# A two-layer encoder on one Trainium2 core: rotary products and weight folds pinned in VectorE's program order, folds in quarters, evictions with priority

## The chip, the core and the metric

The kernel runs on one core of a Trainium2 chip. The core has a matrix engine (TensorE, PE in the profile; its weight loads are listed apart as PEld), a vector engine (VectorE, DVE), a scalar engine (ScalarE, ACT), a slow general engine (GpSimd, POOL) and a sync engine (SyncE, SP), which here only issues DMA transfers. Each engine works through its own list of instructions in order, and the engines wait for one another by semaphores. The metric is the device time of one execution in microseconds (us), the median of several runs.

## What is computed

The reference is a two-layer bidirectional encoder over 272 tokens (16 learned tokens and 256 of input) with a model width of 2048. Cut to what matters:

```python
for i in range(2):
    h = _rmsnorm(h_stream, norm_mix[i])
    proj = h @ w_in[i]                       # q | k | v | f | ga | gf
    q = _rope_2d(_rmsnorm(q, q_norm[i]), ...)
    k = _rope_2d(_rmsnorm(k, k_norm[i]), ...)
    attn = softmax(q k^T / sqrt(128)) v      # 8 query heads, 2 key heads
    a_br = attn @ w_attn_br[i]
    fr = fft2(f by groups of 128 channels, axes=(positions, channels)).real
    s_br = fr @ w_four[i]
    merged = sigmoid(ga) * a_br + sigmoid(gf) * s_br
    h_stream = h_stream + merged @ w_out[i]
    up = _rmsnorm(h_stream, norm_ffn[i]) @ w_up[i]
    u_gate = dwconv3(up[..., :5632]); u_val = up[..., 5632:]
    h_stream = h_stream + (silu(u_gate) * u_val) @ w_down[i]
```

## The kernel before, in words

**Layout.** Activations lie with channels on the 128 partitions and the 272 tokens along the row. Weights come from memory in chunks of 512 KB (`raw`, 128 x 1024 fp32 numbers: four slices of 128 rows by 256 columns), through SyncE's queue at L179 into 4 buffers. Each chunk is split for the matrix engine in two parts, a rounded one and the rest: ScalarE casts `wh` from `raw` (L213), then VectorE computes `wl` = `raw` - `wh` (L214). There are 3 buffers each for `wh` and `wl`. Activations are split in the same way, and PE does three products for each block: `wh` with both activation parts, `wl` with the high one. There are 850 such chunks.

**What runs over what.** `group` (L242 on) works through one block of 256 output columns: for each chunk it splits ahead by two chunks (`LOOK`), then issues the matmuls into accumulators in PSUM, of which the tags `mm` and `aux` have 4 buffers each. Between matmuls, `step` takes one piece of work from a list of generators (`shadow`), which is how the attention, the rotary products and the folds of weights are woven into the stream of matmuls; the numbers that generators yield say how many steps to let pass before the next piece.

**Who decides the order.** The program text is an order of its own, but a scheduler then orders each engine's instructions by priority (by default the place in the text) and by when it reckons an instruction to be ready. A later instruction can therefore be put ahead of an earlier one of the same engine. `tc.keep_in_program_order(ins)` adds a dependence on the instruction of the same engine that stands just ahead in the text, so the instruction cannot be put ahead of that. `tc.high_priority(offset=150)` gives the instructions inside it the priority of a place 150 further up.

**Layer 1's folded projection.** The Fourier branch of layer 1 uses the symmetry of the transform: sums and differences of pairs of weight slices (`fw`, kept in device memory) meet sums and differences of mirrored tokens. `prefold` (L427) makes `fw` beforehand, during the feed-forward part of layer 0: for each of 32 chunks it loads a chunk `pfi` (L433), computes two halves of `pfo`, one sum and one difference of 128 x 512 numbers (L441), and stores `pfo` to `fw` (L435). Both transfers go through SyncE's queue, among the weight chunks. Layer 1 reads `fw` as 16 weight chunks in `folded_f` (L661 on), whose loop over k is the 16 chunks: four groups of two accumulators each (`ps_f`), L679 and L683 for `wh` and `wl`, L682 for a few channels apart. Groups 2 and 3 use the same four PSUM buffers as the q groups. At the last k the accumulators are evicted to `E` (L687, L688). `fold_pair` (L640 to L653) prepares the folded activations `hA` and `hB`, some of them while `folded_f` runs.

**Queries.** The q projection comes in four groups of two heads (i = 0 to 3). In layer 1 the folded projection runs between the second and the third. After each group `head_evac` evicts PSUM: ScalarE squares into `qps` (L745), VectorE scales into `qp` (L746). `q_stage` then takes sums of squares, starts `swap`, four transfers on SyncE's queue (L759) which copy `qp` with its 32-partition blocks exchanged into `qs`, waits some steps and runs `rope`:

- L763: `qs` = `qs` * sin, which needs the four transfers;
- L764: `qp` = `qp` * cos, in place;
- L765: `qp` = `qp` + `qs`;
- L766 on ScalarE and L767 on VectorE: the split of the result into its two parts.

**Attention.** `attention` (L883 on) goes through nine blocks of queries for each key head: scores (L906), maximum (L908), exponential on ScalarE (L913), normalisation on VectorE (L918, L921, L922), transposes on PE (L930) and the products with the values (L952). It begins once the first two q groups are rotated and the Fourier tokens are done, in layer 1 while the third q group and the gates are projected. The exponential needs ScalarE's table loaded, which is a listed instruction of its own at L913. A one-number tile `warm` is written by an activation at the program's start (L374).

Of the kernel before, what the change touches and what calls it, by code (L numbers as in the profile page):

```python
# [2 lines left out]

# [1 line left out]

# [7 lines left out]
AF = mybir.ActivationFunctionType  # L13
ALU = mybir.AluOpType
AX = mybir.AxisListType

P = 128
# [5 lines left out]
KT = D // P  # L23
# [24 lines left out]
TH = T // 2 + 2  # L48
# [13 lines left out]
P_QN = P_BG + DEPTH * 2 * KT  # L62
# [61 lines left out]
def _rep(ap, n):  # L124
    return ap.unsqueeze(1).to_broadcast([ap.shape[0], n, ap.shape[1]])
# [3 lines left out]
def encoder_kernel(ctx, tc, xT, params, consts, bmat, cfold, csign, w_fl, w_f64c, w_in, w_abr, w_four, w_f64, w_out, w_up, w_down, outT):  # L129
    nc = tc.nc  # L130
# [53 lines left out]
    def advance(upto):  # L184
        while st["raw"] < min(upto + RAW, len(chunks)):
            load_raw(st["raw"])
            st["raw"] += 1
        while st["fetch"] < min(upto, len(chunks)):
            i = st["fetch"]
            if i in folded:  # L190
                todo.append((i, lambda i=i: fold_w(i)))
            todo.append((i, lambda i=i: split_w(i, 0, CW)))
            st["fetch"] += 1

    def pump(upto=None):
        if upto is None:
            if todo:
                todo.pop(0)[1]()
        while upto is not None and todo and todo[0][0] <= upto:
            todo.pop(0)[1]()  # L200
# [153 lines left out]
    prm = per.tile([P, P_N], F32, name="prm")  # L354
    cst = per.tile([P, C_N], F32, name="cst")
    ones = per.tile([P, P], F32, name="ones")
    warm = per.tile([P, 1], F32, name="warm")
    mhalf = per.tile([P, 24], F32, name="mhalf")
# [35 lines left out]
    sin = cst[:, C_SIN:C_SIN + T]  # L394
# [7 lines left out]
    def bc2(ap):  # L402
        return _rep(ap, 2)
# [23 lines left out]
    def prefold(pool):  # L427
        src = [w_fl[k] for k in range(KT)] + [w_four[1, j, c] for j in range(NG) for c in range(2)]
        outs = {}
        for j in range(len(src) + 1):  # L430
            if j < len(src):
                a = pool.tile([P, CW, MG * P], F32, tag="pfi", name=f"pfi{j}", bufs=2)
                nc.sync.dma_start(a, src[j])  # L433
            if j:
                nc.sync.dma_start(fw[j - 1], outs.pop(j - 1))  # L435
            yield 12
            if j < len(src):
                o = pool.tile([P, CW, MG * P], F32, tag="pfo", name=f"pfo{j}", bufs=2)
                half = (lambda t_, q: t_[:, :, q * P:(q + 1) * P]) if j < KT else (lambda t_, q: t_[:, 2 * q:2 * q + 2])
                for q, op in ((0, ALU.add), (1, ALU.subtract)):  # L440
                    nc.vector.tensor_tensor(half(o, q), half(a, 0), half(a, 1), op=op)  # L441
                    yield 3
                outs[j] = o
            yield 12

    def norm_stats(holder):
        ps = psum.tile([P, 512], F32, tag="aux", name="ps_nst")
# [25 lines left out]
    for l in range(DEPTH):  # L473
        last = l == DEPTH - 1
        lo = 14 if last else 0
# [4 lines left out]
        with tc.tile_pool(name=f"mix{l}", bufs=1) as mp:  # L480
            E = mp.tile([P, 4, 2, TH] if last else [P, NG, T], F32, tag="q1b" if last else "q1", name="E")
            e64 = mp.tile([2 * NG, TH], F32, tag="u", name="e64", bufs=2) if last else None
# [15 lines left out]
            def rt(name):  # L498
                return mp.tile([P, 2, 2 * TH], F32, tag="r", name=name, bufs=7)[:, :, :T]
# [86 lines left out]
            if l == 0:  # L586
# [18 lines left out]
                ps = group((l, "f", 2), xr(0), T, "aux")  # L605
# [55 lines left out]
            def folded_f(slots, E):  # L661
                assert order[st["grp"]][0] == (l, "f4")
                st["grp"] += 1
                ps = {}
                for g in (0, 1, 2, 3):
                    ps[g] = [psum.tile([P, 512], F32, tag="aux" if g < 2 else "mm", name=f"ps_f{g}{e}") for e in range(2)]
                p64 = ps[0][0][:2 * NG, 2 * TH:3 * TH]
                for k in range(KT):
                    i = st["next"]
                    advance(i + 1 + LOOK)  # L670
                    pump(i)
                    h, lo_ = splits.pop(i)
                    st["next"] += 1
                    sl = slots[k % NS]
                    for g in ((2, 3, 0, 1) if k == KT - 1 else (0, 1, 2, 3)):
                        for e in range(2):
                            w = slice(e * P, (e + 1) * P)
                            o2 = ps[g][e][:, :2 * TH].rearrange("p (r n) -> p r n", r=2)
                            nc.tensor.matmul(o2, h[:, g, w], sl[:, e], start=k == 0, stop=False)  # L679
                            if g == e == 0:  # L680
                                for r in range(2):
                                    nc.tensor.matmul(p64, w64s[:, k, :], sl[:, 0, r, :], start=False, stop=False)  # L682
                            nc.tensor.matmul(ps[g][e][:, :TH], lo_[:, g, w], sl[:, e, 0, :], start=False, stop=k == KT - 1)  # L683
                        pump()
                        if k == KT - 1:
                            for e in range(2):
                                nc.scalar.copy(E[:, g, e, :], ps[g][e][:, TH:2 * TH])  # L687
                                nc.vector.tensor_tensor(E[:, g, e, :], ps[g][e][:, :TH], E[:, g, e, :], op=ALU.add)  # L688
                            if g == 0:
                                nc.scalar.copy(e64, p64)  # L690
                    if k % 2 and k + NS < KT:
                        fold_pair((k + NS - 1) // 2, slots)

# [43 lines left out]
            def head_evac(ps, gcol, name, lo):  # L737
                hp = rt(name)
                sq = rt(name + "s")
                if lo:  # L740
                    nc.gpsimd.memset(hp[:, :, 0:lo], 0.0)
                    nc.gpsimd.memset(sq[:, :, 0:lo], 0.0)
                for m in range(MG):
                    x = ps[m][:, :T - lo]
                    nc.scalar.activation(sq[:, m, lo:T], x, AF.Square)  # L745
                    nc.vector.scalar_tensor_tensor(hp[:, m, lo:T], x, gcol, rstdB[:, lo:T], op0=ALU.mult, op1=ALU.mult)  # L746
                return hp, sq
# [12 lines left out]
                return qs  # L760

            def rope(hp, qs, H, L):
                nc.vector.tensor_tensor(qs, qs, bc2(sin), op=ALU.mult)  # L763
                nc.vector.tensor_tensor(hp, hp, bc2(cos), op=ALU.mult)  # L764
                nc.vector.tensor_tensor(hp, hp, qs, op=ALU.add)  # L765
                nc.scalar.copy(H, hp)  # L766
                nc.vector.tensor_tensor(L, hp, H.bitcast(F32), op=ALU.subtract)  # L767
# [6 lines left out]
            ps = group((l, "k", 0), xr(0), T)  # L774
# [37 lines left out]
            ps = group((l, "v", 0), xr(0), T)  # L812
# [168 lines left out]
            qH, qL = [], []  # L981
            for i in range(4):
                ps = group((l, "q", i), xr(lo), W)
                qq = head_evac(ps, prm[:, P_QN + l:P_QN + l + 1], "qp", lo)
                if last:
                    if i in (0, 2):
                        until(hold, "vt" if i == 0 else "fold")
                        for t_, n in ((qH, "q1"), (qL, "q2")):
                            t_.append(mp.tile([P, 4, T], F32R, tag=n + "ab"[i // 2], name=n))
                elif i == 0:  # L990
                    until(hold, "vt")
                    until(hold, "fold")
                    for t_, n in ((qH, "q1"), (qL, "q2")):
                        t = mp.tile([P, NH, T], F32R, tag=n, name=n)
                        t_ += [t[:, 0:4], t[:, 4:8]]
                push(q_stage(i, *qq), 4)
                if last and i == 1:
                    until(hold, "ahead")
                    folded_f(slots, E)
                    o1_tiles()  # L1000
                    push(folded_chan(E), 1)
# [14 lines left out]
            for half in range(2):  # L1016
                mH = mL = None
                for kind, i in BRANCH_ORDER[half]:
                    j = i - 4 * half
# [18 lines left out]
                    else:  # L1038
# [6 lines left out]
                        ps = group((l, "a", i), lambda kt: (qH[kt // 4][:, kt % 4, lo:T], qL[kt // 4][:, kt % 4, lo:T]), W)  # L1045
                        for m in range(MG):
                            k = 2 * j + m
                            t_, h_ = tha[i][:, m, lo:T], mH[:, k, lo:T]
# [4 lines left out]
                for mg in range(8):  # L1053
                    ps = group((l, "o", half, mg), lambda kt: (mH[:, kt, lo:T], mL[:, kt, lo:T]), W)
# [7 lines left out]
        with tc.tile_pool(name=f"ffn{l}", bufs=1) as fp:  # L1062
# [6 lines left out]
            for c, n in enumerate(FF_SPLIT):  # L1069
                gHL = fp.tile([P, FF_SPLIT[0], 2, T], F32R, tag="gHL", name="gHL")  # L1070
                gH, gL = gHL[:, :, 0, :], gHL[:, :, 1, :]
                for i in range(k0 // MG, (k0 + n) // MG):
                    ps = group((l, "ug", i), xr(lo), W)
                    until(hold, "tok2")
                    cs = []
                    for m in range(MG):
# [7 lines left out]
                        a = max(lo2, 1)  # L1084
# [5 lines left out]
                    ps = group((l, "uv", i), (lambda kt: (xHL[:, kt, :, lo2:T],)) if fused else xr(lo2), W2)  # L1090
                    for m in range(MG):
                        j = 2 * i + m - k0
# [11 lines left out]
                for mg in range(8):  # L1104
                    two = fused and not (lastc and mg == 7)
                    ps = group((l, "d", c, mg), (lambda kt: (gHL[:, kt, :, lo2:T],)) if two
                               else (lambda kt: (gH[:, kt, lo2:T], gL[:, kt, lo2:T])), W2)
# [78 lines left out]
```

## Time and profile before

| what | us |
|---|---|
| median of three runs | 2589.75 |
| lowest and highest of the three | 2589.42, 2589.86 |
| the profiled execution, its own time | 2590.24 |
| span of the profiled execution (first to last instruction) | 2588.5 |
| one cast `wh` (L213), mean of 850 | 1.046 |
| one `wl` (L214), mean of 850 | 1.222 |
| memory traffic over the span | 493 MB, 191 GB/s |

How to read the views: a row of a timeline is the start in us, the duration in us, the engine, the line, the operation, the tiles written and read with their shapes, and in brackets the time for which the engine stood idle before it and what ended that. A row of a list of groups gives the count, the busy time and the mean of one instruction in ns, and then the idle time before them. A row of a list of waits gives the engine and line that waited, the engine and line that ended the wait, and the total, the number and the longest of these waits. "Granted clock" is the share of full speed at which PE was allowed to run.

### The profile page before, as it was taken

The page shows a single profiled execution, that of the slowest core. Times are in us where ns is not written, and L with a number is a line of the kernel's source. Part 1 is how long each engine was busy: PE and PEld are TensorE (multiplying, and loading weights), DVE is VectorE, ACT ScalarE, POOL GpSimd, SP SyncE. Part 2 cuts the span into 40 slices and gives each one's busy share as a digit, 9 for nine tenths or more (in the row PEclk, how much of TensorE's full clock was granted, in tenths as well). Part 3 has the DMA queues.
Part 4 walks back from the last instruction along what each step waited for, and adds up shares of the span by engine and source line. Part 5 has one row for each costly group of instructions (what it writes and reads, how often), then busy time and mean ns, then how long its engine had stood idle before and what let it go on. Part 6 is the DMA issues. An engine that isn't in the chain of part 4 may idle for free.

```text
span 2588.5 us, 47816 instructions
## 1 busy us (share of the span) xinstructions
PE 2570.9 (99%) x19604; PEld 2503.6 (97%) x19604; DVE 1720.3 (66%) x2742; ACT 1215.5 (47%) x1762; POOL 19.5 (1%) x40
## 2 busy tenths in 40 slices
PE   9999999999999999999999999999999999999999
PEld 9999999999999999999998999999999998899988
DVE  7787766777765445565567777667766665566654
ACT  5455434554444334444445555445544543354443
POOL 0000000000000000000000000000000000000000
PEclk9999999999999999999999999999999999999999
DMA  7545555589985555555556446566555555555564
GB/s 234 168 148 164 186 183 186 183 288 323 315 284 178 173 178 171 178 173 177 173 164 206 146 146 199 189 194 191 184 184 187 187 187 188 187 183 186 186 199 158
DMA packets 142811, 499.20 MB, mean 193 GB/s; under 512 B 16368, under 2 KB 23152, under 8 KB 142592
## 3 DMA queue, kind: packets, MB, share of 16 engines
q1 hardware_dynamic: 140144, 494.02, 58.1%
q8 instruction: 153, 2.51, 0.4%
q10 hardware_dynamic: 2448, 2.13, 0.2%
q14 instruction: 66, 0.54, 0.1%
HBM read 474.43 MB, written 18.87 MB: 191 GB/s over the span
## 4 chain that ended last, share of the span: by engine, by line
PE 92%; DVE 3%; DMA 3%; ACT 1%; issue 1%; SPq 0%; POOL 0%; DVEq 0%; ACTq 0%
PE ps_uv L266 6%; PE ps_ug L271 6%; PE ps_ug L272 6%; PE ps_ug L270 6%; PE ps_d L266 6%; PE ps_d L270 4%; PE ps_d L271 4%; PE ps_d L272 4%; PE ps_uv L267 3%; PE ps_d L267 3%; PE ps_uv L272 3%; PE ps_uv L270 3%; PE ps_uv L271 3%; PE ps_gf L270 2%; PE ps_gf L271 2%; PE ps_o L271 2%
## 5 line engine op out<-in xcount | busy, mean ns | idle before, releaser
L214 DVE TENSOR_TENSOR wl<-raw,wh 128x1024 fp32r<-128x1024 f32 (+1 forms) x850 | 1036.1, 1222 | 676.7 <-ACT wh L213 671.0
L213 ACT CAST wh<-raw 128x1024 fp32r<-128x1024 f32 (+1 forms) x850 | 887.7, 1046 | 989.9 <-issue 156.3
L271 PE MATMUL ps_ug<-xHL,wh 128*128 128x272 f32 (+1 forms) x1408 | 402.4, 286 | 0.0
L272 PE MATMUL ps_ug<-xHL,wl 128*128 128x272 f32 (+1 forms) x1408 | 402.2, 286 | 0.1
L270 PE MATMUL ps_ug<-xHL,wh 128*128 128x272 f32 (+1 forms) x1408 | 402.0, 286 | 0.0
L270 PEld LDWEIGHTS ps_ug<-xHL,wh 128*128 128x128 f32 x1408 | 265.4, 189 | 1.0
L272 PEld LDWEIGHTS ps_ug<-xHL,wl 128*128 128x128 f32 x1408 | 265.0, 188 | 0.7 <-DVE wl L214 0.7
L271 PEld LDWEIGHTS ps_ug<-xHL,wh 128*128 128x128 f32 x1408 | 265.5, 189 | 0.1
L266 PE MATMUL ps_uv<-xHL,wh 128*128 128x512 f32 x704 | 247.7, 395 | 0.0
L266 PE MATMUL ps_d<-gHL,wh 128*128 128x512 f32 x664 | 233.1, 395 | 0.0
L271 PE MATMUL ps_d<-gHL,wh 128*128 128x272 f32 (+1 forms) x744 | 214.4, 288 | 0.0
L270 PE MATMUL ps_d<-gHL,wh 128*128 128x272 f32 (+1 forms) x744 | 214.1, 288 | 0.0
L272 PE MATMUL ps_d<-gHL,wl 128*128 128x272 f32 (+1 forms) x744 | 214.0, 288 | 0.0
L272 PE MATMUL ps_uv<-xHL,wl 128*128 128x272 f32 x704 | 203.2, 289 | 0.6 <-DVE wl L214 0.5
L271 PE MATMUL ps_uv<-xHL,wh 128*128 128x272 f32 x704 | 203.0, 288 | 0.0
L270 PE MATMUL ps_uv<-xHL,wh 128*128 128x272 f32 x704 | 202.9, 288 | 0.0
L267 PE MATMUL ps_uv<-xHL,wl 128*128 128x256 f32 x704 | 197.7, 281 | 0.0
L267 PE MATMUL ps_d<-gHL,wl 128*128 128x256 f32 x664 | 186.5, 281 | 0.0
L266 PEld LDWEIGHTS ps_uv<-xHL,wh 128*128 128x128 f32 x704 | 132.4, 188 | 29.9
L266 PEld LDWEIGHTS ps_d<-gHL,wh 128*128 128x128 f32 x664 | 125.0, 188 | 29.2
L270 PE MATMUL ps_ga<-xHL,wh 128*128 128x272 f32 (+1 forms) x512 | 148.0, 289 | 0.0
L270 PE MATMUL ps_gf<-xHL,wh 128*128 128x272 f32 (+1 forms) x512 | 147.3, 288 | 0.0
(321 smaller groups left out, 5854.7 us busy)
## 6 DMA issues: line engine op xcount, KB each, us to landing
raw<-in_w_up SPq DMA_DIRECT2D x352, 512.0 KB, 3.5
raw<-in_w_in SPq DMA_DIRECT2D x191, 512.0 KB, 3.6
raw<-in_w_down SPq DMA_DIRECT2D x176, 512.0 KB, 3.5
raw<-in_w_out SPq DMA_DIRECT2D x64, 512.0 KB, 3.5
raw<-in_w_abr SPq DMA_DIRECT2D x32, 512.0 KB, 3.5
fw<-pfo SPq DMA_DIRECT2D x32, 512.0 KB, 6.4
raw<-fw SPq DMA_DIRECT2D x32, 512.0 KB, 3.6
raw<-in_w_four SPq DMA_DIRECT2D x16, 512.0 KB, 3.7
```

Of the source, the lines that this page charges most:

```text
L213: nc.scalar.copy(h[:, a:b], r[:, a:b])
L214: nc.vector.tensor_tensor(lo[:, a:b], r[:, a:b], h[:, a:b].bitcast(F32), op=ALU.subtract)
L266: nc.tensor.matmul(o2, h[:, c, sl], ab, start=kt == 0, stop=False)
L267: nc.tensor.matmul(o, lo[:, c, sl], ab[:, 0, :], start=False, stop=kt == nk - 1)
L270: nc.tensor.matmul(o, h[:, c, sl], a, start=kt == 0, stop=False)
L271: nc.tensor.matmul(o, h[:, c, sl], b, start=False, stop=False)
L272: nc.tensor.matmul(o, lo[:, c, sl], a, start=False, stop=kt == nk - 1)
```

## The change

It has five parts: `prefold` works in quarters (128 x 256 numbers) in place of halves, each one pinned, with other numbers of steps between the pieces; the evictions to `E` and, for the second q group of layer 1, those of `head_evac` stand under `high_priority`; the first rotary product is pinned; and an exponential on the one-number tile `warm` is issued at k = 2 of `folded_f`.

```diff
--- before.py
+++ after.py
@@ -1,5 +1,5 @@
 import math
-from contextlib import ExitStack
+from contextlib import ExitStack, nullcontext
 
 import numpy as np
 
@@ -433,15 +433,16 @@
                 nc.sync.dma_start(a, src[j])
             if j:
                 nc.sync.dma_start(fw[j - 1], outs.pop(j - 1))
-            yield 12
+            yield 15
             if j < len(src):
                 o = pool.tile([P, CW, MG * P], F32, tag="pfo", name=f"pfo{j}", bufs=2)
-                half = (lambda t_, q: t_[:, :, q * P:(q + 1) * P]) if j < KT else (lambda t_, q: t_[:, 2 * q:2 * q + 2])
                 for q, op in ((0, ALU.add), (1, ALU.subtract)):
-                    nc.vector.tensor_tensor(half(o, q), half(a, 0), half(a, 1), op=op)
-                    yield 3
+                    for c in range(2):
+                        half = (lambda t_, e: t_[:, 2 * c:2 * c + 2, e * P:(e + 1) * P]) if j < KT else (lambda t_, e: t_[:, 2 * e + c])
+                        tc.keep_in_program_order(nc.vector.tensor_tensor(half(o, q), half(a, 0), half(a, 1), op=op))
+                        yield 3
                 outs[j] = o
-            yield 12
+            yield 1
 
     def norm_stats(holder):
         ps = psum.tile([P, 512], F32, tag="aux", name="ps_nst")
@@ -683,11 +684,14 @@
                             nc.tensor.matmul(ps[g][e][:, :TH], lo_[:, g, w], sl[:, e, 0, :], start=False, stop=k == KT - 1)
                         pump()
                         if k == KT - 1:
-                            for e in range(2):
-                                nc.scalar.copy(E[:, g, e, :], ps[g][e][:, TH:2 * TH])
-                                nc.vector.tensor_tensor(E[:, g, e, :], ps[g][e][:, :TH], E[:, g, e, :], op=ALU.add)
-                            if g == 0:
-                                nc.scalar.copy(e64, p64)
+                            with tc.high_priority(offset=150):
+                                for e in range(2):
+                                    nc.scalar.copy(E[:, g, e, :], ps[g][e][:, TH:2 * TH])
+                                    nc.vector.tensor_tensor(E[:, g, e, :], ps[g][e][:, :TH], E[:, g, e, :], op=ALU.add)
+                                if g == 0:
+                                    nc.scalar.copy(e64, p64)
+                    if k == 2:
+                        nc.scalar.activation(warm, mhalf[:, 0:1], AF.Exp)
                     if k % 2 and k + NS < KT:
                         fold_pair((k + NS - 1) // 2, slots)
 
@@ -760,7 +764,7 @@
                 return qs
 
             def rope(hp, qs, H, L):
-                nc.vector.tensor_tensor(qs, qs, bc2(sin), op=ALU.mult)
+                tc.keep_in_program_order(nc.vector.tensor_tensor(qs, qs, bc2(sin), op=ALU.mult))
                 nc.vector.tensor_tensor(hp, hp, bc2(cos), op=ALU.mult)
                 nc.vector.tensor_tensor(hp, hp, qs, op=ALU.add)
                 nc.scalar.copy(H, hp)
@@ -981,7 +985,8 @@
             qH, qL = [], []
             for i in range(4):
                 ps = group((l, "q", i), xr(lo), W)
-                qq = head_evac(ps, prm[:, P_QN + l:P_QN + l + 1], "qp", lo)
+                with tc.high_priority(offset=150) if last and i == 1 else nullcontext():
+                    qq = head_evac(ps, prm[:, P_QN + l:P_QN + l + 1], "qp", lo)
                 if last:
                     if i in (0, 2):
                         until(hold, "vt" if i == 0 else "fold")
```

## The prediction

> **What bounds the kernel now.** I read the busy table first.
>
> ```profile
> span 2588.5 us, 47816 instructions
> PE 2570.9 (99%) x19604; PEld 2503.6 (97%) x19604; DVE 1720.3 (66%) x2742; ACT 1215.5 (47%) x1762; POOL 19.5 (1%) x40
> ```
>
> TensorE (PE) is busy in all but 2588.5 − 2570.9 = 17.6 us of the span. The change removes no matmul, so it can win from PE's idle time, and from time in which PE runs at a lower clock. VectorE (DVE), at 66%, matters only where PE waits for it. The second view is the list of PE's waits.
>
> ```profile
> PE ps_f L338 <- ACT wh L213: 4.7, 2, 4.5
> PE ps_f L683 <- DVE wl L214: 3.7, 2, 3.3
> PE ps_pt L930 <- DVE pn L921: 1.6, 1, 1.6
> PE ps_f L679 <- DVE qp L746: 1.5, 1, 1.5
> PE ps_pv L952 <- DVE PL L944: 0.5, 1, 0.5
> PE ps_q L270 <- DVE E L688: 0.5, 1, 0.5
> ```
>
> The columns are total us, times and longest us. The first row is the start of the program, which the diff does not touch. Rows two to four, 6.8 us, lie in layer 1's folded projection and the first attention step behind it. I looked at these stretches by window: length, busy time of PE (with its matmuls), PEld, DVE, ACT and POOL, then the granted clock.
>
> ```profile
> 1408.00:1412.00 4.00, 1.04 (x10) 0.81 (x8) 2.25 (x3) 0.00 (x0) 0.00 (x0) 1.00 0.32 109
> 1412.00:1414.00 2.00, 1.70 (x13) 1.70 (x14) 1.23 (x3) 1.03 (x2) 0.12 (x1) 0.93 0.36 86
> 1414.00:1420.30 6.30, 5.87 (x27) 5.29 (x27) 3.96 (x4) 3.77 (x6) 0.00 (x0) 0.50 0.57 196
> 1420.30:1426.00 5.70, 5.70 (x49) 5.64 (x49) 3.20 (x3) 3.01 (x9) 0.00 (x0) 0.98 0.64 238
> 1466.00:1470.00 4.00, 2.38 (x21) 2.21 (x20) 3.53 (x12) 1.92 (x9) 0.00 (x0) 1.00 0.81 217
> ```
>
> After the wait around 1410, PE runs at half clock. A mean of 0.93 over 2 us puts the drop 0.28 us before 1414.00, at 1413.72; 0.98 over 5.7 us puts the return 0.23 us after 1420.30, at 1420.53. At half clock for 6.8 us, PE does 3.4 us less work than it could; some 0.3 us of that falls on a second short wait, so the clock costs about 3.1 us. No idle-time row shows this term. The stall at 1466 to 1470, of 1.6 us, left the clock at 1.00.
>
> **The change part by part.** The order in which the changed program's instructions stand on each engine differs from the diff's wording in two places, and I cost the order.
>
> *Eviction of q 1 (high priority on `head_evac`).*
>
> ```profile
> 1385.37 1.23 DVE L214 TENSOR_TENSOR wl<-raw,wh 128x1024 fp32r<-128x1024 f32 x1
> 1386.51 0.72 DVE L767 TENSOR_TENSOR q<-qp,q 128x544 fp32r<-128x544 f32 x1
> 1387.15 0.48 DVE L746 SCALAR_TENSOR_TENSOR qp<-ps_q,prm,rstdB 128x258 f32<-128x258 f32 x1
> 1387.68 0.39 PE L679 MATMUL ps_f<-hA,wh 128*128 128x276 f32 x1 [1.53 <-DVE qp L746]
> ```
>
> The last accumulator of `folded_f` needs the bank that the second L746 empties, and that stands behind L767. Its order now is wl, L746, L767: L746 starts 1387.15 − 1386.51 = 0.64 us sooner. But the scheduler also swaps one pair on PE: the first matmul of the next k, which PE did ahead of the wait before, now stands behind the matmul that waits, so a little of the work that filled the time is left over (one or two matmuls of 0.2 to 0.4 us). I take 0.3 (0 to 0.65).
>
> *Rotary products.* The intent is to keep products off VectorE's queue until their data is there. The rows at k = 11 of `folded_f`:
>
> ```profile
> 1408.74 0.29 PE L682 MATMUL ps_f<-hA,w64s 128*16 128x138 f32 x2
> 1412.30 0.33 PE L683 MATMUL ps_f<-hA,wl 128*128 128x138 f32 x1 [3.27 <-DVE wl L214]
> ...
> 1404.70 0.50 DVE L652 SCALAR_TENSOR_TENSOR hB<-hf,prm,hB 128x276 fp32r<-128x276 f32 x1
> 1409.75 0.73 DVE L763 TENSOR_TENSOR qs<-qs,cst 128x544 f32<-128x544 f32 x1 [4.55 <-DMA qs<-qp]
> 1410.39 0.72 DVE L764 TENSOR_TENSOR qp<-qp,cst 128x544 f32<-128x544 f32 x1
> 1411.03 1.22 DVE L214 TENSOR_TENSOR wl<-raw,wh 128x1024 fp32r<-128x1024 f32 x1
> 1412.16 0.72 DVE L765 TENSOR_TENSOR qp<-qp,qs 128x544 f32<-128x544 f32 x1
> 1413.65 0.72 DVE L767 TENSOR_TENSOR q<-qp,q 128x544 fp32r<-128x544 f32 x1 [0.77 <-ACT q L766]
> 1414.60 2.57 DVE L214 TENSOR_TENSOR wl<-raw,wh 128x1024 fp32r<-128x1024 f32 x2 [0.22 <-PE ps_f L679]
> ```
>
> VectorE stands 4.55 us at L763 until the four transfers qs<-qp (L759) land, with the `wl` that PE needs behind it. Only L763 is pinned. In the changed program L764, unpinned, stands in L763's old place, ahead of that same `wl`. It overwrites qp, which the four transfers read, so it waits for all four; L763 comes later and waits for nothing. **The wait passes from L763 to L764 and is not removed.** Queued behind it are the two `wl` of the next chunks, and behind these PE. What goes is one product in front of `wl` (1410.39 − 1409.75 = 0.64) and L765, L766 and L767 between the two `wl`. So `wl` starts at 1410.39, PE resumes 0.64 sooner, its wait falls from 3.27 to 2.63, and the second wait of L683 (3.7 − 3.3 = 0.4) goes, since the next `wl` follows directly. Together 1.0 us (0.4, if the second wait stays half and the landing slips a little, to 1.7, if the transfers land earlier by what the q eviction gains and more).
>
> Whether the clock still drops is the largest unknown here, since no row shows a wait of 2.6 us: a wait of 3.27 us was followed by half clock, ones of 1.53 and 1.62 us were not. By the nearest row 2.63 lies nearer to 3.27 (0.64 away, against 1.0). I take it that the drop stays: 0 of the 3.1 us gained (0 to 3.1).
>
> The Trainium skill, page "TensorE: Matmul & The Clock Gate", section "What's actually happening", has the clock halved after an idle window of about 3.4 us, in windows that run freely; its section "Why this matters for your kernels" asks for no idle gaps above about 3 us. The trace agrees in the length, 6.8 us being two such windows, and by that rule a gap of 2.6 us would not be throttled. But the rule's window was not wholly idle here: between 1410.3 and 1413.7, 3.4 us before the drop, PE worked from 1412.30 on, so the trace has a partly busy window throttled. By the rule the sum would be 3.1 us lower, by my reading of the row it stays.
>
> *The first attention step.* L763, L765 and L767 of the third q group also leave their place.
>
> ```profile
> 1456.17 0.72 DVE L763 TENSOR_TENSOR qs<-qs,cst 128x544 f32<-128x544 f32 x1 [3.53 <-DMA qs<-qp]
> 1460.08 0.72 DVE L767 TENSOR_TENSOR q<-qp,q 128x544 fp32r<-128x544 f32 x1 [0.41 <-ACT q L766]
> 1466.41 1.21 DVE L214 TENSOR_TENSOR wl<-raw,wh 128x1024 fp32r<-128x1024 f32 x1
> 1464.80 1.28 ACT L913 ACT_TABLE_LOAD   x1
> 1466.66 0.57 ACT L913 ACTIVATE pe<-ps_s,nb,rq 128x272 f32<-128x272 f32 x1
> 1468.34 0.35 DVE L921 TENSOR_SCALAR pn<-pe,rs 128x256 f32<-128x256 f32 x1
> 1468.83 0.52 PE L930 MATMUL ps_pt<-cst,pn 128*128 128x128 f32 x3 [1.62 <-DVE pn L921]
> ```
>
> PE waits 1.62 us for L921, which stands behind the `wl` of 1466.41. Ahead of that `wl` VectorE loses three products at 0.64 start to start and the 0.41 us wait, 2.3 us in all, so it is no longer late: the `wl` goes as soon as its cast `wh` is there (just before 1464.80, where the table load begins), ends near 1466.1, and L754 with the reductions puts L921 at about 1467.5. Transposes would start near 1467.6 instead of 1468.83, so 1.2 (0 to 1.6). The added `warm` exponential has no inputs and stands at the front of ScalarE's program in the built order; the table load of L913 remains where it is, so this edit gains nothing, and costs one small activation that the 4.5 us wait of the start covers. The moved products stand later in the attention, behind L938, where VectorE idled.
>
> *Folds of the weights.*
>
> ```profile
> L441 DVE TENSOR_TENSOR pfo<-pfi x64: 683/686/695, 539.5 to 750.6; 128x512 f32<-128x512 f32 x64
> ...
> L644 DVE TENSOR_TENSOR hf<-t 128x274 f32<-128x274 f32 x1 | 0.4, 445 | 0.0
> ...
> DVE pfo L441 <- DMA pfi<-in_w_four: 26.7, 15, 3.8
> PEld ps_uv L272 <- DVE wl L214: 1.5, 4, 0.5
> PEld ps_ug L272 <- DVE wl L214: 0.7, 3, 0.3
> ```
>
> From 640 to 760 us VectorE waits 26.7 us, up to 3.8 at a time, for transfers of weights to be folded, and `wl` splits behind it come late: PE's weight loads wait 1.5 + 0.7 = 2.2 us. The changed program keeps each fold some eight chunks behind its transfer on the sync queue and spreads the 32 folds over more than 200 chunks instead of about 65, so I take all 2.2 (−1 to 2.2). The quarters, 128 of 128x256, have no row; by the 128x274 row at 445 ns one is at most 0.445 and, from half of the halves' 0.69, at least 0.34 us: at 0.43, 128 × 0.43 = 55 us against 64 × 0.69 = 44, so 11 us more VectorE work, some 0.05 us per chunk, hidden in its 34% idle time; without that cover it would cost those 11 us. The folded weights are read only in layer 1, far behind the last fold.
>
> *Evictions E.* They keep their order: 0; the 0.5 us at L270 stays. Layer 0's q groups change in the same way; their stalls, such as the 0.5 at L952, may move: 0 (−0.5 to 0.5).
>
> Sum: 0.3 + 1.0 + 1.2 + 2.2 = 4.7 us. The profiled execution took 2590.24 us (span 2588.5 and 1.7 around it), so 2585.5. It is 0.5 us above the runs' median 2589.75; against that, **2585.0**.
>
> **The rivals.** *The clock does not drop.* For it: 2.63 us is well under 3.27, and the two waits below it did no harm. Against: a window around the drop was 41% busy (1412.30 to 1413.72 out of 3.4 us), and a gap of 2.63 leaves at worst 0.8 of 3.4, 23%, busy. Time 2585.0 − 3.1 = 2581.9. This is also what the rule quoted above gives.
>
> *The change does what it says,* VectorE never standing at a rotary product in the fold: then the remaining 2.63 go too, 2581.9 − 2.6 = 2579.3. Against it: L764's waits in the program.
>
> *The folds give nothing back,* because PE's waits in ffn 0 come from the traffic and casts and not from the folds' queue: 2585.0 + 2.2 = 2587.2.
>
> *The inherited wait moves into the attention (slower).* One mechanism: L764 of the third and fourth q group stands at its transfers with the attention's reductions, L908 and L921, behind it.
>
> ```profile
> DVE qs L763 <- DMA qs<-qp: 8.1, 2, 4.5
> ```
>
> Before, L763 waited twice from 1380 to 1480 us, 4.55 and 3.53 us, and only the first hit PE. If each hits PE as at k = 11 (3.3 + 0.4 and 3.1 of clock), that is 2 × 6.8 = 13.6: 2585.0 + 13.6 = 2598.6. It decides once VectorE gets to L764 more than 3.5 us ahead of the landing, for that much cost PE nothing in the third group. Against: the fourth group had no such wait at all (the 8.1 us are the two others).
>
> **How the numbers follow.** Forecast 0.55, clock kept 0.22, what it says 0.05, folds idle 0.09, slower 0.09. The forecast's own range is 2583 to 2587, by the terms' bounds not all at one end. For 8 in 10 I reach down to the kept clock with a little more won, 2580.0, and up over the idle folds, 2589.5. About 0.2% (5.2 us, below 2584.6 or above 2594.9) is what can be told from no change. Faster: 0.4 of the forecast's 0.55, and 0.27 of the next two: 0.49. Slower: 0.08, same 0.43.
>
> **What would show it.** L764, not L763, with an idle time for DMA qs<-qp of some 4.5 us in the fold and 3.5 in the third group; PE's longest wait at L683 near 2.6 us and a half clock behind it; the wait at L930 under 0.6; L746 ahead of L767, with PE's L679 waiting 0.9 to 1.3; no wait of the folds for pfi and PEld waits at L272 gone from ffn 0; L913's table load still there in layer 1. I am wrong if the clock stays at 1.00 through the fold, if PE shows new waits behind quarter folds, or if L764 waits inside the attention with PE behind it.

## The result and the profile after

The changed kernel took 2584.10 us (median of 10 runs, 2581.81 to 2586.82) against 2589.82 for the kernel before on the same chip (median of 10 runs). The ratio is 0.9973, with a 95% interval of 0.9963 to 0.9983: 0.27% faster, about 0.9 us below the forecast of 2585.0 and inside its range.

The page of the profiled execution, which took 2586.43 us, begins with the span and the busy times:

```profile
span 2584.7 us, 47878 instructions
PE 2569.7 (99%) x19604; PEld 2504.6 (97%) x19604; DVE 1725.5 (67%) x2806; ACT 1216.5 (47%) x1763; POOL 19.4 (1%) x40
```

PE's idle time fell from 17.6 to 15.0 us with the same number of matmuls. VectorE has 64 instructions more, and ScalarE one. The list of PE's waits (total, times, longest) answers to the one before; the changed file's lines lie one to four further down, so L683 is now L684, L746 is L750 and L930 is L934:

```profile
PE ps_f L338 <- ACT wh L213: 5.9, 2, 4.5
PE ps_f L684 <- DVE wl L214: 2.6, 1, 2.6
PE ps_f L680 <- DVE qp L750: 1.2, 1, 1.2
PE ps_pv L956 <- DVE PL L948: 0.8, 1, 0.8
PE ps_q L270 <- DVE E L690: 0.5, 1, 0.5
PE ps_pt L934 <- DVE pn L925: 0.3, 1, 0.3
```

Every wait that the change meant to shorten is shorter, and the long one in the folded projection (now L684) is still there. The waits at the program's start (first row) and in layer 0's attention (L956, 0.5 us before) are longer. The timeline shows why the long one stayed. These are VectorE's rows around it, with PE's row at the end:

```profile
1403.39 0.50 DVE L653 SCALAR_TENSOR_TENSOR hB<-hf,prm,hB 128x276 fp32r<-128x276 f32 x1
1408.43 0.72 DVE L768 TENSOR_TENSOR qp<-qp,cst 128x544 f32<-128x544 f32 x1 [4.53 <-DMA qs<-qp]
1409.07 3.49 DVE L214 TENSOR_TENSOR wl<-raw,wh 128x1024 fp32r<-128x1024 f32 x3
...
1410.34 0.48 PE L684 MATMUL ps_f<-hA,wl 128*128 128x138 f32 x1 [2.56 <-DVE wl L214]
```

VectorE waits 4.53 us for the swap's transfers, as it did before (4.55 us), but at the second product, qp * cos (L764 before, L768 now), which overwrites what the transfers read. Behind it three splits `wl` follow at once, where before one rotary product stood ahead of the first and two others behind it. So PE's wait is 0.71 us shorter, and the second, short one has gone.

The windows below (length; PE, PEld, DVE, ACT and POOL busy with their counts; the granted clock; the transfers) are cut at the clock's changes:

```profile
1406.88:1410.30 3.42, 0.90 (x9) 0.67 (x7) 1.87 (x3) 1.04 (x1) 0.00 (x0) 1.00 0.40 133
1410.30:1413.71 3.41, 3.37 (x15) 3.37 (x16) 2.26 (x2) 0.00 (x0) 0.00 (x0) 0.50 0.68 189
1413.71:1417.13 3.42, 3.42 (x18) 3.34 (x18) 1.23 (x1) 1.05 (x1) 0.00 (x0) 0.50 0.74 277
1417.13:1420.54 3.41, 3.41 (x31) 3.35 (x31) 1.23 (x1) 1.97 (x2) 0.00 (x0) 1.00 0.49 154
```

After a wait of 2.56 us PE again ran at half clock for 6.83 us: 15 and 18 matmuls in 3.4 us, then 31. That costs 3.4 us.

At the first attention step the table load is where it was, and the wait is nearly gone (rows of the timeline of ScalarE, VectorE and PE):

```profile
2.70 0.20 ACT L694 ACTIVATE warm<-mhalf 128x1 f32<-128x1 f32 x1
...
1462.25 1.28 ACT L917 ACT_TABLE_LOAD   x1
1464.52 0.35 DVE L925 TENSOR_SCALAR pn<-pe,rs 128x256 f32<-128x256 f32 x1
1465.02 0.52 PE L934 MATMUL ps_pt<-cst,pn 128*128 128x128 f32 x3 [0.30 <-DVE pn L925]
```

The first row is the added exponential: it runs 2.70 us after the start of the program, 1380 us before the place in the text where it was written.

The folds, in the list of the instructions that touch `pfo`, with what they waited for:

```profile
L442 DVE TENSOR_TENSOR pfo<-pfi x128: 414/418/424, 554.5 to 1214.7; 128x256 f32<-128x256 f32 x128
```

No wait for `pfi` stands under it any more (before: 26.7 + 13.9 us in the same list), and PE has no wait at L272 in the feed-forward part. The folds are spread over 660 us (554.5 to 1214.7) instead of 211. In the stretch that held them before, PE now gets through 20 matmuls more (the profile before first, then the one after):

```profile
520.00:760.00 240.00, 239.33 (x1892) 237.66 (x1891) 182.80 (x276) 109.20 (x147) 1.22 (x1) 1.00 0.90 313
520.00:760.00 240.00, 240.00 (x1912) 239.92 (x1911) 161.61 (x255) 111.27 (x148) 0.85 (x1) 1.00 0.68 222
```

### The profile page after: what moved, and what is told of

It is laid out like the page before. It is cut to its first block, busy times and chain, and to the rows that moved or that the text cites. A ratio compares the mean times of both kernels' runs of the same rounds, so it can differ in the third digit from the quotient of the medians.

```text
span 2584.7 us, 47878 instructions
## 1 busy us (share of the span) xinstructions
PE 2569.7 (99%) x19604; PEld 2504.6 (97%) x19604; DVE 1725.5 (67%) x2806; ACT 1216.5 (47%) x1763; POOL 19.4 (1%) x40
## 4 chain that ended last, share of the span: by engine, by line
PE 98%; DVE 1%; DMA 0%; ACT 0%; issue 0%; SPq 0%; DVEq 0%; ACTq 0%
PE ps_ug L271 7%; PE ps_ug L270 7%; PE ps_ug L272 7%; PE ps_uv L266 6%; PE ps_d L266 6%; PE ps_d L270 4%; PE ps_d L271 4%; PE ps_d L272 4%; PE ps_uv L270 3%; PE ps_uv L271 3%; PE ps_uv L272 3%; PE ps_uv L267 3%; PE ps_d L267 3%; PE ps_gf L270 2%; PE ps_gf L271 2%; PE ps_o L271 2%
## 5 line engine op out<-in xcount | busy, mean ns | idle before, releaser
L272 PE MATMUL ps_ug<-xHL,wl 128*128 128x272 f32 (+1 forms) x1408 | 401.9, 285 | 0.0
L272 PEld LDWEIGHTS ps_ug<-xHL,wl 128*128 128x128 f32 x1408 | 265.0, 188 | 0.0
L272 PE MATMUL ps_d<-gHL,wl 128*128 128x272 f32 (+1 forms) x744 | 214.0, 288 | 0.0
L272 PE MATMUL ps_uv<-xHL,wl 128*128 128x272 f32 x704 | 202.8, 288 | 0.0
```

What stands on the lines that cost most here:

```text
L272: nc.tensor.matmul(o, lo[:, c, sl], a, start=False, stop=kt == nk - 1)
```

## The experiments

Each kernel was timed in turn with the kernel before on the same chip. That kernel's median moved between 2589.8 and 2591.5 us from one set of runs to the next, so ratios are compared first.

**Both products pinned.** One line on top of the change:

```diff
-                nc.vector.tensor_tensor(hp, hp, bc2(cos), op=ALU.mult)
+                tc.keep_in_program_order(nc.vector.tensor_tensor(hp, hp, bc2(cos), op=ALU.mult))
```

> The changed kernel with the second product, qp * cos, pinned as well. Theory (the wait for the four transfers passed from the first product to the second): with both pinned VectorE no longer stands at a transfer inside the folded projection, the 2.6 us wait of PE's L684 goes and with it the half clock behind it, so the time falls by 2.7 us of stall and up to 3.4 us of clock below the changed kernel, to 2578 to 2581. Rival (the splits wl were late for their own casts or weight transfers, and the product only stood in the gap): the wait at L684 stays above 2 us, the time within 1 us of the changed kernel. Rival (the products, now both in the attention, make its transposes wait): L684's wait goes, but waits at L934 or L956 grow by 2 us or more and take half of it back.

Measured: 2578.24 us (2577.53 to 2579.55), ratio 0.9950 (0.9937 to 0.9964). All of its waits of PE behind the start are:

```profile
PE ps_f L680 <- DVE qp L750: 1.2, 1, 1.2
PE ps_q L270 <- DVE E L690: 0.5, 1, 0.5
PE ps_pt L934 <- DVE pn L925: 0.2, 1, 0.2
PE ps_nb L466 <- DVE tok L469: 0.2, 1, 0.2
```

The windows over the same stage of the folded projection:

```profile
1404.00:1408.00 4.00, 4.00 (x36) 3.94 (x36) 2.34 (x2) 2.27 (x3) 0.00 (x0) 1.00 0.99 339
1408.00:1412.00 4.00, 4.00 (x37) 3.94 (x37) 2.56 (x3) 2.19 (x3) 0.00 (x0) 1.00 0.72 240
```

PE is busy throughout, at full clock. The step from the changed kernel, 5.9 us by the medians, is the 2.6 us of the wait and the 3.4 us of clock. No wait came up in the attention; the one at L956, in layer 0's attention, went as well. The theory holds, both rivals fall.

**The second product not in place.** Is it the position of this product or what it overwrites? Here it stays unpinned, and writes to the tile of the squares:

```diff
-                nc.vector.tensor_tensor(hp, hp, bc2(cos), op=ALU.mult)
-                nc.vector.tensor_tensor(hp, hp, qs, op=ALU.add)
+                nc.vector.tensor_tensor(hc, hp, bc2(cos), op=ALU.mult)
+                nc.vector.tensor_tensor(hp, hc, qs, op=ALU.add)
...
-                rope(qp, qs, qH[kv][:, sl, :], qL[kv][:, sl, :])
+                rope(qp, qs, qH[kv][:, sl, :], qL[kv][:, sl, :], qsq)
```

The keys' products are changed in the same way (not shown).

> The changed kernel, with the second product, unpinned as there, written to the tile of the squares, which is free by then, so that it overwrites nothing that the four transfers read. Theory (the overwriting alone makes it wait): no wait of VectorE for qs<-qp in the folded projection, the 2.6 us wait at PE's L684 and the half clock gone, within 1 us of the 2578.2 of both products pinned. Rival (the position of the product matters, whatever it writes): the wait at L684 stays above 1.5 us and the time above 2581.

Measured: 2578.37 us (2577.80 to 2580.51), ratio 0.9954 (0.9941 to 0.9966). VectorE has no wait for `qs<-qp` anywhere, PE none at L684. With nothing overwritten, the unpinned product did no harm here. But the scheduler also put it much later in VectorE's order, at 1424.12 us, behind all the splits of the folded projection, instead of 1408.43 in the changed kernel. So the run does not separate the two causes: that the product would have waited for no transfer wherever it stood follows from the program, which no longer overwrites what the transfers read, and not from this measurement.

**The folds alone,** put into the kernel before.

> The kernel before with the new folds alone (quarters, pinned, other numbers of steps). Theory: PE's weight loads no longer wait at L272 in the feed-forward part of layer 0, 2.2 to 2.4 us gained, so about 2587.4; the 3.3 us wait in the folded projection and its half clock stay as they are. Rival (the folds give nothing back, PE's waits there are of the casts and the traffic): within 0.5 us of before, and waits at L272 between 650 and 750 us remain.

Measured: 2587.11 us (2585.78 to 2588.25, 11 runs) against 2591.52 (2586.48 to 2596.81, 27 runs), ratio 0.9982 (0.9974 to 0.9991). No waits at L272 are left; the wait in the folded projection is 2.9 us, with the half clock behind it. By the medians the folds are worth 4.4 us (2.3 to 6.7 by the interval) and not 2.2, and the runs lie within 2.5 us of one another where those of before spread over 10. The folds in two other forms, further below, show where the spread comes from.

**The first product pinned alone,** in the kernel before.

> The kernel before with the first rotary product pinned, and nothing else. Theory: the longest wait at L683 falls from 3.3 to about 2.6 us, the second one goes, and the wait at the first transposes falls from 1.6 to below 0.6: 0.7 + 0.7 + 1.2 = 2.6 us, so about 2587.2; if the clock no longer drops behind the shorter wait, some 3 us more, 2584. Rival (in the changed kernel it is the earlier q eviction and not the pin that shortens the waits): within 0.5 us of before.

Measured: 2586.91 us (2583.00 to 2591.05), ratio 0.9984 (0.9976 to 0.9993). The wait at the first transposes is 0.2 us, the second wait at L683 is gone, and the first is 2.08 us. The rival falls. The clock is the surprise of this run. PE's row in the timeline, then the windows:

```profile
1412.28 0.34 PE L683 MATMUL ps_f<-hA,wl 128*128 128x138 f32 x1 [2.08 <-DVE wl L214]
```

```profile
1409.12:1412.54 3.42, 1.34 (x12) 1.12 (x12) 2.18 (x3) 1.04 (x1) 0.00 (x0) 1.00 0.30 104
1412.54:1415.95 3.41, 3.41 (x18) 3.33 (x18) 1.95 (x2) 0.38 (x1) 0.00 (x0) 0.50 0.74 239
1415.95:1419.36 3.41, 3.41 (x32) 3.38 (x30) 1.61 (x2) 1.71 (x2) 0.00 (x0) 1.00 0.76 241
```

A wait of only 2.08 us was followed by half clock, this time for 3.41 us.

**The priority of the q evictions alone,** in the kernel before.

> The kernel before with the priority for the evictions of the second q group alone. Theory: one wait, at L679, falls from 1.5 to 1.2 us, so 0.3 us gained, 2589.5, which the timing cannot tell from no change. Rival (the earlier eviction starts the swap's transfers earlier too, and so shortens the 3.3 us wait): 0.6 us or more gained, and L763's wait below 4.3 us.

Measured: 2589.71 us (2587.51 to 2593.77), ratio 0.9996 (0.9987 to 1.0005): no change that could be told. The wait at L679 fell to 1.2 us as in the changed kernel. L763's waits come to 7.6 us in two, the longer 3.9 us, 0.6 below before's, and PE's longest wait behind the start is 3.1 us. A wait below 4.3 us is what the rival named; but VectorE's wait there varies as much in kernels that leave these evictions alone (3.2 us in the folds-only kernel, where PE's is 2.9), so one profile does not decide it. Nor does the time: its interval reaches from 3.4 us gained to 1.3 lost, and holds the 0.3 us of the theory and the 0.6 of the rival alike. This profile shows something else. Its folds are those of before, and VectorE waited for them:

```profile
L441 DVE TENSOR_TENSOR pfo<-pfi x64: 678/685/695, 540.2 to 748.3; 128x512 f32<-128x512 f32 x64
  DMA pfi<-in_w_four: 13.8, 14
  DMA pfi<-in_w_fl: 12.0, 9
```

Yet no wait of PE or of its loads at L272 is listed. VectorE waited 25.8 us here and 40.6 in the profile before.

**The folds in quarters, not pinned,** and **the folds in halves, pinned,** both at the steps of the change, each in the kernel before. The edit of the first is shown against the change's folds, that of the second against the folds before:

```diff
-                        tc.keep_in_program_order(nc.vector.tensor_tensor(half(o, q), half(a, 0), half(a, 1), op=op))
+                        nc.vector.tensor_tensor(half(o, q), half(a, 0), half(a, 1), op=op)
```

> The kernel before with the folds in quarters at the steps of the change, but not pinned. Theory (the pin makes the gain): VectorE waits 20 us or more for pfi again, PE waits at L272 by turns of 0 to 3 us from run to run, the time near before's and as scattered. Rival (the size or the steps make it): as the folds-only kernel, 2587.1, with runs within 2.5 us of one another.

```diff
-            yield 12
+            yield 15
...
-                    nc.vector.tensor_tensor(half(o, q), half(a, 0), half(a, 1), op=op)
-                    yield 3
+                    tc.keep_in_program_order(nc.vector.tensor_tensor(half(o, q), half(a, 0), half(a, 1), op=op))
+                    yield 6
...
-            yield 12
+            yield 1
```

> The kernel before with the folds as halves, but pinned, at the steps of the change. Theory (the place makes the gain, not the size): no waits of VectorE for pfi, no waits of PE at L272 in the feed-forward part, the time within 0.7 us of the folds-only kernel's 2587.1. Rival (a half of 0.69 us in front of a split is too long): waits at L272 of 1 us or more remain in that part, 2588 or more.

Measured: quarters not pinned 2590.57 us (2588.07 to 2594.69), ratio 0.9997 (0.9989 to 1.0006); pinned halves 2587.97 (2586.59 to 2589.65), ratio 0.9989 (0.9980 to 0.9998). The list of waits of VectorE and of PE's loads in the kernel with loose quarters:

```profile
DVE pfo L442 <- DMA pfi<-in_w_four: 23.4, 11, 3.8
DVE pfo L442 <- DMA pfi<-in_w_fl: 16.2, 9, 3.1
...
PEld ps_uv L272 <- DVE wl L214: 3.3, 4, 1.2
PEld ps_ug L272 <- DVE wl L214: 0.3, 1, 0.3
```

Without the pin no gain is left that could be told; with it and in halves there is no such wait. The interval of the pinned halves overlaps that of the pinned quarters (0.9974 to 0.9991). In the four profiles with loose folds the loads' waits at L272 came to 2.2 (before), 2.0 (first product pinned alone), 0.0 (evictions alone) and 3.6 us: the loss varies from one profile to the next.

What this is worth shows in PE's own progress. From the start of the matmul behind the first 4000 to that of the one behind the first 7000 (509 to 889 us before) the time is:

| profile | us |
|---|---|
| each of the eight with pinned folds, quarters or halves | 376.88 |
| evictions alone (loose halves) | 376.99 |
| before (loose halves) | 379.45 |
| first product pinned alone (loose halves) | 379.59 |
| loose quarters | 381.00 |

So loose folds cost from 0.1 to 4.1 us in these profiles, and with the pin the size of the pieces makes no difference in this stretch. Pinned folds with the old numbers of steps were not run, so whether the new numbers are needed as well is not shown.

The same kernel's profile gave a second case for the clock: two waits, of 3.19 and 2.02 us, of which the first was followed by half clock and the second was not. First PE's row for the second, then the windows:

```profile
1469.86 0.52 PE L931 MATMUL ps_pt<-cst,pn 128*128 128x128 f32 x3 [2.02 <-DVE pn L922]
```

```profile
1411.26:1414.68 3.42, 0.26 (x2) 0.26 (x3) 2.81 (x4) 0.00 (x0) 0.00 (x0) 1.00 0.08 30
1414.68:1418.09 3.41, 3.41 (x18) 3.33 (x18) 2.30 (x4) 3.00 (x6) 0.12 (x1) 0.50 0.51 154
...
1465.87:1469.28 3.41, 1.96 (x17) 1.76 (x15) 3.37 (x10) 2.11 (x5) 0.00 (x0) 1.00 0.73 254
1469.28:1472.70 3.42, 2.84 (x24) 2.87 (x25) 2.65 (x12) 1.39 (x4) 0.00 (x0) 1.00 0.68 203
```

The last two windows are cut sixteen steps of 3.413 us behind the drop at 1414.68. Cut there, the wait of 2.02 us falls into two windows, 1.96/3.41 = 57% and 83% busy.

**Without the warm exponential.**

> The changed kernel without the exponential on the warm tile. Theory (it stands at the front of ScalarE's program and does nothing): within 0.5 us of the changed kernel's 2584.1, the table load of L913 in layer 1 in the same place, the wait at the first transposes again near 0.3 us. The wait in the folded projection stays near 2.6 us, and a half clock of 3.4 or 6.8 us follows it whenever most of it falls in one window. Rival (the activation helps or hurts the start or the attention): 1 us or more apart.

Measured: 2585.58 us (2583.30 to 2587.02), ratio 0.9980 (0.9971 to 0.9989), against 0.9973 (0.9963 to 0.9983) with it: the intervals overlap, no difference is shown, though the medians, from two different sets of runs, lie 1.5 us apart and not within 0.5. Behind the first 4000 matmuls the two profiles gain nearly the same on the kernel before, 5.2 us without the exponential and 5.3 with it; what is left between them lies ahead of that, where the first 50 matmuls alone vary by 2 us from profile to profile, so an effect on the start is not excluded. The wait at the first transposes is 0.3 us again, the one in the folded projection 3.0 us, with half clock behind it.

**Both products pinned, and the exponential too.**

```diff
-                        nc.scalar.activation(warm, mhalf[:, 0:1], AF.Exp)
+                        tc.keep_in_program_order(nc.scalar.activation(warm, mhalf[:, 0:1], AF.Exp))
```

> The changed kernel with both products pinned and the exponential on the warm tile pinned too, so that the table load leaves the attention for the third chunk of the folded projection. Theory: the load was in front of the first exponential, but with both products pinned only 0.2 us of wait is left at the first transposes, so at most 0.3 us below the 2578.2 of both products pinned, and the clock at 1.00 throughout. Rival (a load of 1.3 us in front of a cast wh in the folded projection makes wl late there): a new wait at L684 of 0.5 us or more, 2579 or more.

Measured: 2577.86 us (2577.50 to 2578.63), ratio 0.9950 (0.9937 to 0.9962). Now the load is where the text has it:

```profile
L694 ACT ACT_TABLE_LOAD  x1: 1283/1283/1283, 1387.7 to 1387.7; - x1
```

The wait at the transposes is gone, none came at L684. The 0.4 us between the two medians lies inside their runs' spread.

**The next chunk's matmuls in the last wait.** On top of that, the order of the first two chunks of the folded projection:

```diff
+                units = [(k, g) for k in range(KT) for g in ((2, 3, 0, 1) if k == KT - 1 else (0, 1, 2, 3))]
+                units[:8] = [(0, 0), (0, 1), (0, 2), (1, 0), (1, 1), (1, 2), (0, 3), (1, 3)]
```

> Both products and the warm exponential pinned, and in the folded projection the first three groups of the second chunk's matmuls put ahead of the first chunk's fourth group, which needs the bank that the second q group's last eviction empties. Theory (PE only lacks work while that eviction stands behind a split): the wait of 1.1 to 1.2 us at L680 goes, 2576.8, no new wait. Rival (the first chunk's wh and wl are held longer, so a split two chunks on comes late): the wait at L680 goes and one of 0.5 us or more appears at L684, 2577.5 or more.

Measured: 2577.51 us (2577.19 to 2578.29), ratio 0.9950 (0.9936 to 0.9963). PE's waits in the folded projection:

```profile
PE ps_f L689 <- DVE wl L214: 0.7, 1, 0.7
PE ps_q L270 <- DVE E L696: 0.5, 1, 0.5
```

The wait for the eviction (1.1 us) is gone, and one of 0.7 us for a split has come in its place, as the rival said: the chunk held longer, or the split itself, is late next. The 0.35 us that are left cannot be told apart by these runs. This kernel is at 0.9950 of the kernel before, like the two others with both products pinned, and all three beat the change.

## Why the prediction was right, point by point

**The q eviction** was taken at 0.3 us: the wait at L679 went from 1.53 to 1.21 us (at L680). Right, and alone it does not show in the time.

**The rotary products** were the main step. That the wait passes from the first product to the second and is not removed is shown by the row of L768 with its 4.53 us and by pinning it; the run that lets it write elsewhere agrees, but moved it too. Expected were a wait of 2.63 us in place of 3.27 and the end of the second one, 1.0 us; measured 2.56 and none, 1.1 us.

**The clock** was expected to drop again, and did. The reason given, that 2.63 us is nearer to 3.27 than to 1.62, is not what decides: 2.08 us was enough in one kernel, and 2.02 us was not in another. What tells the cases apart is how busy PE was in the stretch of 3.41 us that ends at the drop: 41% before (1.41/3.41 in the window named in the prediction), 26% after (0.90/3.42), 39% and 8% in the two kernels above, and 57% in the stretch without a drop. The prediction had this share beside its rival (41% before, at worst 23% after) but did not decide by it. So the rival "the clock does not drop" lay less in the length of the wait than in where it falls. Among the ten runs of the change the two fastest, 2581.81 and 2583.14 us, are the only ones whose mean granted clock is listed as 1.000 and not 0.999. One drop of 3.41 us is already listed as 0.999 (first product pinned alone), so these two runs probably had none, and that rival came true in them; no trace of them is here to show it. A third run took 2583.16 us with 0.999, so the drop alone does not order the runs. That the profile, and by this listing eight runs of ten, went with the forecast is in part luck. The term was sized at 3.1 us before. It is rather 3.2, since the 0.43 us in which PE idled at half clock would have given 0.2 us of work and not 0.3, and it is 3.4 after, where PE hardly waits inside the half-clock stretch.

**The first attention step** was taken at 1.2 us: 1.62 went to 0.30, 1.3 us. No gain of the exponential is shown, as costed; pinned, it does move the load, and by then there is nothing left to win from that.

**The folds** were taken at 2.2 us, the waits of PE's weight loads. PE's own list before has less at that line:

```profile
PE ps_uv L272 <- DVE wl L214: 0.5, 2, 0.3
```

Loads run while matmuls run (PE is busy in 99% and PEld in 97% of the span), so neither list is the price by itself; by the progress of PE it was 379.45 − 376.88 = 2.57 us in this pair of profiles. The mechanism is right (the pin removes the waits), but a loss that differs from profile to profile was read as a fixed one: loose folds cost 0.1 to 4.1 us, and the folds alone moved the median by 4.4 us. One quarter takes 418 ns, as estimated (0.43).

**The rivals.** "The change does what it says" was priced at 2579.3 and is the kernel with both products pinned, 2578.24. The slower one, an inherited wait inside the attention, did not come: the third group's 3.95 us at L768 again cost PE nothing.

**The sum.** Both profiles list 19604 matmuls, so they can be compared by when PE starts the matmul behind the same number of others. Behind the first 4000 the later profile is 1.50 us late. It then gains 2.57 us up to 7000 (the folds), nothing up to 10900, 0.31 up to 11000 (the eviction), 1.09 up to 11400 (the rotary products, with the clock), 1.35 up to 12000 (the first attention step), and nothing more: 5.3 us gained where the prediction has 4.7. Less the 1.5 us, this is the 3.8 us by which the spans differ. Of the 1.5 us, 1.4 arise in the first 50 matmuls, which the diff does not touch: the waits for casts there come to 5.9 us in place of 4.7, and matmuls of one shape start 0.23 us apart until 14.3 us in place of 10.8, and 0.13 apart from then on. That start varies: the 50 are through between 14.9 and 16.9 us in the twelve profiles, and the kernel before was profiled with the earliest. So the forecast came within 0.9 us of the median partly by luck: the start varies by 2 us and the loose folds by 4.

## What to carry to other kernels

Where a wait is to be taken out of an engine's order, list every instruction that waits for the same event, those that overwrite what a transfer still reads among them: moving one leaves the next to inherit the wait. Work at the side that has slack belongs pinned where its data is sure to be there; left to the scheduler, the folds were placed ahead of their transfers' landing (25.8 to 44.1 us of waits in the four profiles with loose folds), and the loss then varied from 0.1 to 4.1 us. A stall of TensorE of 2 to 3 us can cost twice its length or more when the clock drops behind it (2.56 and 3.4 us here), so taking out the last part of it is worth more than shortening it.

## What the runs showed of the hardware

Behind the program's start, the granted clock dropped after every stall of 2.56 us and more that these profiles hold, after one of 2.08 us, and not after one of 2.02 us. Within a profile the listed changes of the clock lie whole steps of 3.413 us apart (before: 10.83 to 1413.71 us is 411.0 steps). Cut in these steps, every stretch ahead of a drop in the folded projection was at most 41% busy, and none that was 57% busy or more had a drop behind it; between the two these profiles have no case.

The half clock lasted 6.83 us in six profiles and 3.41 us in two. In these two the whole stretch behind the drop was busy (18 matmuls in it, 3.41 us of 3.41). But that does not decide it: in the kernel with pinned halves that stretch is listed as wholly busy too (3.42 us of 3.42, 17 matmuls), and the clock stayed low for a second one, as it did after the change with 3.37 of 3.41 us. What brings the clock back after one stretch is not shown.

The Trainium skill, page "TensorE: Matmul & The Clock Gate", section "What's actually happening", has a window of 3413 ns that runs freely; the length agrees (3.41 and 6.83 us). Its halving "after ≥1 idle window" does not: stretches with 26 to 41% of busy time were halved here, and one with 57% was not.
